# A quadrant-swapping copy in HBM: one queue of sixteen DMAs, or two queues of sixteen smaller ones

## The chip, the core and the metric

The kernel runs on one core of one Trainium2 chip. The metric is device time in microseconds for one execution. The core's instruction streams are those of TensorE (PE), VectorE (DVE), ScalarE (ACT), GpSimd (POOL) and SyncE (SP). Data between tensors in HBM is moved by the core's 16 DMA engines, which work through DMAs that one of the instruction streams has put on a queue.

## What is computed

```python
def setup_inputs():
    return {
        "x": np.random.randn(8192, 8192).astype(np.float32),
    }

def reference(x: np.ndarray) -> np.ndarray:
    return np.fft.ifftshift(x)
```

For an even size, `ifftshift` swaps the four quadrants of the matrix crosswise: the upper left quarter of the output is the lower right quarter of the input, the upper right is the lower left, and so on. Nothing is calculated. The matrix has 8192 rows of 32 KiB, 268.44 MB in all; each quadrant has 4096 rows, and a quadrant's part of a row is 4096 floats, 16 KiB, contiguous in memory. The next row of the same quadrant lies 32 KiB further on.

## The kernel before

The kernel consists of DMAs from the input in HBM straight to the output in HBM. The list `quads` (lines 23 to 28) names the four quadrants of the output, each with the quadrant of the input that it comes from. The outer loop (line 33) takes them in the order upper left, upper right, lower left, lower right. The inner loop (line 36) cuts each into `nsplit = 4` strips of 1024 rows, and line 41 issues one DMA for each strip: 16 DMAs of 1024 x 4096 floats, 16 MiB each.

`engines = [nc.sync]` (line 30) has one entry, so every DMA is issued by SP, in program order, on one queue. The other engines hold nothing but start and end barriers and, on POOL, four tiny constant fills.

The DMAs don't depend on each other. Tile, the layer in which the kernel is written, gives each a semaphore on which its landing is counted. There are eight of them, dealt out in turn, so the ninth DMA is issued only when the first has landed, the tenth when the second has, and so on. At the end of the program SP waits until the last DMAs have landed.

Of the kernel before, what the change touches and what calls it, by code (L numbers as in the profile page):

```python
# [1 line left out]

# [4 lines left out]


@with_exitstack  # L10
def kernel(
    ctx: ExitStack,
    tc: tile.TileContext,
    x: bass.AP,
    out: bass.AP,
):
    nc = tc.nc

    R, C = x.shape
    hr = R // 2  # L20
    hc = C // 2

    quads = [
        ((0, hr), (0, hc), (hr, R), (hc, C)),
        ((0, hr), (hc, C), (hr, R), (0, hc)),
        ((hr, R), (0, hc), (0, hr), (hc, C)),
        ((hr, R), (hc, C), (0, hr), (0, hc)),
    ]

    engines = [nc.sync]  # L30
    nsplit = 4
    k = 0
    for (or0, or1), (oc0, oc1), (ir0, ir1), (ic0, ic1) in quads:
        rows = or1 - or0
        step = rows // nsplit
        for s in range(nsplit):
            a = s * step
            b = a + step
            eng = engines[k % len(engines)]
            k += 1  # L40
            eng.dma_start(
                out=out[or0 + a : or0 + b, oc0:oc1],
                in_=x[ir0 + a : ir0 + b, ic0:ic1],
            )


# [1 line left out]
_INS = ['x']  # L48
_OUTS = [((8192, 8192), 'float32')]


def kernel(**inputs):
    import numpy as _np
    import concourse.bacc as _bacc
    import concourse.tile as _tile
    from concourse import mybir as _mybir
    from concourse.bass_utils import run_bass_kernel_spmd as _run

    nc = _bacc.Bacc("TRN2", target_bir_lowering=False, num_devices=1)  # L59
    arrays, args = {}, []  # L60
    for name in _INS:
        a = _np.ascontiguousarray(inputs[name])
        if a.dtype.kind in "iu":
            a = a.astype(_np.int64)
        arrays[f"in_{name}_dram"] = a
        args.append(nc.dram_tensor(f"in_{name}_dram", a.shape, _mybir.dt.from_np(a.dtype), kind="ExternalInput").ap())
    for i, (shape, dtype) in enumerate(_OUTS):
        dt = _mybir.dt.from_np(_np.dtype(dtype))
        args.append(nc.dram_tensor(f"out_{i}_dram", shape, dt, kind="ExternalOutput").ap())
    with _tile.TileContext(nc) as tc:  # L70
        kernel(tc, *args)
    r = _run(nc, [arrays], core_ids=[0])
    got = tuple(r.results[0][f"out_{i}_dram"] for i in range(len(_OUTS)))
    return got[0]
```

## Time and profile before

| What | Value |
|---|---|
| Median of 5 runs | 813.25 us (810.6 to 817.13) |
| The profiled execution, its own time | 813.76 us |
| The profiled execution, span from first to last instruction | 812.0 us |
| Instructions in the span | 61 |
| Busy time of compute engines | POOL 0.2 us, others none |
| DMA packets | 16,640 |

The page of the profile has a line `DMA` that shows how busy the 16 DMA engines were in each of 40 equal slices of the span (9 stands for 90% or more), and a line `GB/s` with what they moved in it, counted once for a byte that is read and written. A DMA is carried out as packets, and the part on the DMA queues gives for each queue its packets, their bytes in MB, and the time that the packets took, as a share of 16 engines over the whole span. The part on DMA issues gives, for each line of the kernel, the number of DMAs, the size of one, and the median time from issue to landing. Instructions that issue DMAs aren't counted as busy.

### The profile page before, as it was taken

Reading aid. Unit: us, or ns where it says so; the run is one execution under the profiler, and the core shown is the slowest. Engines: PE = TensorE matmul, PEld = TensorE weight load, DVE = VectorE, ACT = ScalarE, POOL = GpSimd, SP = SyncE. Lnnn points to the kernel's source line nnn. Section 1 sums busy time; section 2 is a strip of 40 time slices with the busy share of each in tenths; the row PEclk is TensorE's granted clock in tenths of the full one; section 3 lists DMA queues with packets and bytes.
Section 4 is the critical chain, followed back from the end, with each engine's and each line's share of the span. In section 5 each row is a group of like instructions: output and inputs, shape, how many; then the busy total and the mean of one; then the engine's idle time right before and its main releaser. Section 6 shows DMA issues by size and latency. Waiting matters only on the chain. (4 is left out here: it accounts for less than half of the span.)

```text
span 812.0 us, 61 instructions
## 1 busy us (share of the span) xinstructions
POOL 0.2 (0%) x4
## 2 busy tenths in 40 slices
POOL 0000000000000000000000000000000000000000
DMA  9999999999999999999999999999999999999998
GB/s 298 318 319 328 330 333 332 334 338 333 338 324 338 333 336 335 337 331 328 334 337 337 335 333 335 335 337 328 335 333 329 333 341 330 334 337 334 334 333 278
DMA packets 16640, 268.44 MB, mean 331 GB/s; under 512 B 256, under 2 KB 256, under 8 KB 256
## 3 DMA queue, kind: packets, MB, share of 16 engines
q1 hardware_dynamic: 16640, 268.44, 99.2%
HBM read 268.44 MB, written 268.44 MB: 661 GB/s over the span
## 5 line engine op out<-in xcount | busy, mean ns | idle before, releaser
L59 POOL MEMSET const-bfloat16-1.0<- 128x1 bf16 x1 | 0.1, 101 | 0.0
L59 POOL MEMSET const-uint8-127<- 128x1 uint8 x1 | 0.1, 101 | 0.0
L59 POOL MEMSET const-float32-0.0<- 128x1 f32 x1 | 0.1, 98 | 0.2 <-issue 0.2
L59 POOL MEMSET const-float32-1.0<- 128x1 f32 x1 | 0.1, 98 | 0.0
## 6 DMA issues: line engine op xcount, KB each, us to landing
out_dram<-in_x_dram SPq DMA_DIRECT2D x16, 16384.0 KB, 157.2
```

The costliest lines, as they stand in the source:

```text
L59: nc = _bacc.Bacc("TRN2", target_bir_lowering=False, num_devices=1)
```

## The change

The list of quadrants and the loop over it are replaced by a loop over strips of 512 rows of the upper half, and within it over the two column halves. Each step issues two DMAs. SP's writes 512 rows of the upper half of the output, from the lower half of the input. ScalarE's (`nc.scalar`) writes 512 rows of the lower half of the output, from the upper half of the input; where SP's writes the left columns it writes the right ones, and the other way round. A strip is 512 x 4096 floats, 8 MiB, and there are 32 DMAs, 16 on each of two queues.

```diff
+ROWS_PER_DMA = 512
...
-    quads = [
-        ((0, hr), (0, hc), (hr, R), (hc, C)),
-        ((0, hr), (hc, C), (hr, R), (0, hc)),
-        ((hr, R), (0, hc), (0, hr), (hc, C)),
-        ((hr, R), (hc, C), (0, hr), (0, hc)),
-    ]
-
-    engines = [nc.sync]
-    nsplit = 4
-    k = 0
-    for (or0, or1), (oc0, oc1), (ir0, ir1), (ic0, ic1) in quads:
-        rows = or1 - or0
-        step = rows // nsplit
-        for s in range(nsplit):
-            a = s * step
-            b = a + step
-            eng = engines[k % len(engines)]
-            k += 1
-            eng.dma_start(
-                out=out[or0 + a : or0 + b, oc0:oc1],
-                in_=x[ir0 + a : ir0 + b, ic0:ic1],
+    for row in range(0, hr, ROWS_PER_DMA):
+        for col in (0, hc):
+            other = hc - col
+            nc.sync.dma_start(
+                out=out[row : row + ROWS_PER_DMA, col : col + hc],
+                in_=x[row + hr : row + hr + ROWS_PER_DMA, other : other + hc],
+            )
+            nc.scalar.dma_start(
+                out=out[row + hr : row + hr + ROWS_PER_DMA, other : other + hc],
+                in_=x[row : row + ROWS_PER_DMA, col : col + hc],
             )
```

The eight landing semaphores are dealt out in turn over the DMAs of both queues: SP and ScalarE get four each, and from its fifth DMA on each of the two waits, before it issues, until the DMA that it issued four earlier has landed.

## The prediction

> **What bounds the kernel now.** No engine computes anything here, so I read the page's DMA lines first, then the DMA share by stretch of time, and then the waits of the sync engine's queue. The page:
>
> ```profile
> span 812.0 us, 61 instructions
> DMA  9999999999999999999999999999999999999998
> GB/s 298 318 319 328 330 333 332 334 338 333 338 324 338 333 336 335 337 331 328 334 337 337 335 333 335 335 337 328 335 333 329 333 341 330 334 337 334 334 333 278
> q1 hardware_dynamic: 16640, 268.44, 99.2%
> HBM read 268.44 MB, written 268.44 MB: 661 GB/s over the span
> out_dram<-in_x_dram SPq DMA_DIRECT2D x16, 16384.0 KB, 157.2
> ```
>
> One queue, q1, keeps the 16 DMA engines occupied for 99.2% of the span, and every slice but the last is at nine tenths or more. The chain of waits is of no use: it follows engine instructions and ends after 0.4 us. Of the 16,640 packets, 256 are the small ones that report a landing (16 DMAs on 16 engines); the other 16,384 carry 16 KiB each, one row of a quadrant, since 268.44 MB / 16,384 = 16,384 bytes. A packet therefore holds an engine for 0.992 x 16 x 812.0 / 16,384 = 0.787 us, which is 20.8 GB/s an engine and 333 GB/s for 16.
>
> Does something leave these engines without work, or do they work slower than they could? The windows (their first line names the columns):
>
> ```profile
> core 0: us, POOL busy (x), PEclk, DMA share, GB/s
> 0.00:5.00 5.00, 0.20 (x4) 1.00 0.61 223
> 5.00:20.00 15.00, 0.00 (x0) 1.00 1.00 321
> 20.00:60.00 40.00, 0.00 (x0) 1.00 1.00 319
> 60.00:110.00 50.00, 0.00 (x0) 1.00 0.99 330
> 110.00:160.00 50.00, 0.00 (x0) 1.00 1.00 333
> 210.00:410.00 200.00, 0.00 (x0) 1.00 1.00 333
> 610.00:790.00 180.00, 0.00 (x0) 1.00 1.00 334
> 805.00:812.00 7.00, 0.00 (x0) 1.00 0.55 176
> ...
> 3.00:4.00 1.00, 0.00 (x0) 1.00 1.01 426
> 302.00:303.00 1.00, 0.00 (x0) 1.00 1.09 426
> 305.00:306.00 1.00, 0.00 (x0) 1.00 0.74 279
> ```
>
> The share is 0.99 to 1.00 from 5 us to the tail, so no engine waits for descriptors, not even where one 16 MB DMA ends and the next begins. The last windows are of single microseconds: the rate swings between 279 and 426 GB/s while its mean stays at 333. The engines can thus run at 426 for a moment (26.6 GB/s an engine, 0.615 us a packet) and are held back to 0.787 us by something that they share. The stretch up to 60 us, in which all 16 have just started together, is the slowest: 319 to 321. The sync engine's own waits:
>
> ```profile
> SPq L70 <- DMA out_dram<-in_x_dram: 108.9, 3, 50.3
> ```
>
> These 108.9 us are its wait for the last landings. It issues far ahead (157.2 us from issue to landing, three DMAs of some 50 us). The issue takes nothing from the path.
>
> **What the Trainium skill says.** *HBM Reference*, Specifications: a pair of cores has about 716 GB/s of memory bandwidth. The trace's 661 GB/s, read and written together, is 92% of that, which agrees with memory, not the engines, as the shared limit. *DMA: Bandwidth & Descriptors*, "Issuing engines are not separate DMA queues": DMAs from scalar and sync run on the same 16 engines and interleave, and a second issuer saves only sequencer time. This trace has one issuer and can't show interleaving; it does show that there is no sequencer time to save. The same page, "Queues, rings and completion order": an engine takes turns between the rings that have work, a packet at a time. The same page, "Latency and other measured facts": streams that run in lock step with address pitches of large powers of two lose bandwidth (164 GB/s a direction at a pitch of 2 MiB, 207 at 512 KiB). No run here shows a pitch, but the slow first 60 us is what one would see if engines in step disturbed each other.
>
> **The change, part by part.**
> - Bytes and packets. Every output quadrant is still copied from the opposite one in rows of 16 KiB: 16,384 data packets, the same 268.44 MB each way. Landing packets go from 256 to 512 (32 DMAs x 16 engines). I take such a packet as under 0.1 us, since the share shows no dip at DMA ends; 16 more an engine are then at most 1.6 us, probably far less: 0 to +1.6, taken as +0.2.
> - Sync engine. It issues 16 DMAs of 8 MB in place of 16 of 16 MB. They lie beside the transfers now and do so after. Without that cover each issue would cost about 0.6 us (the first in the trace took 0.58), some 9 us in all.
> - Scalar engine. It gets 16 issues on a queue that was empty. The one thing exposed is its first issue, and until it has packets the sync ring feeds all 16 engines: 0.
> - Added waits. The eight landing semaphores are dealt out in turn over both issuers, so each has four, and its fifth DMA waits until its first has landed (before: the ninth for the first). Behind it in that queue stand only later DMAs. Three DMAs of 32 packets an engine are still queued in each ring, together 6 x 32 x 0.787 = 151 us of work. Cost 0; if it failed, one refill of about 2 us (the trace's first data moved at 2 us) at each of 12 waits would be 24 us, yet the other ring would have to be dry as well.
> - End. The rings share each engine, so one ending first leaves the whole engine to the other. The tail (share 0.55 over 7 us: 3.2 us) stays.
> - Order of addresses. This is the part that the trace of before can't price. Now all engines read one quadrant and write one; an engine's successive packets are 32 KB apart in both. After, an engine alternates between two quadrants read and two written, 128 MiB and one 16 KiB half row apart, and the block of one engine within a DMA (if rows are divided evenly and in order) falls from 64 rows, 2 MiB, to 32 rows, 1 MiB. Bound below: memory at the page's full 716 GB/s moves 536.9 MB in 750 us, and with what the engines don't fill (0.8% of 812.0: 6.5 us) it ends at 756. Bound above, by the nearest row, the 319 GB/s of the disturbed start held throughout: 268.44 / 0.319 = 841.5, and 6.5 makes 848. I take +1 us: the memory is already at 92% with 16 packets moving at once, and 16 still move at once whichever ring they come from; a slight loss is likelier to me than a gain, as four regions are open in place of two.
>
> Sum: 812.0 + 0.2 + 1 = 813.2 for the span. What lies around it is 813.76 - 812.0 = 1.8 us, so 815. The profiled run is 0.5 us above the median of 813.25, which is less than the spread of the five runs; I leave 815.
>
> **The rivals.**
> 1. *More open regions, worse memory efficiency: slower.* For: the engines already swing from 279 to 426[...], and a start in step costs 4% (319 against 333), so order matters. Against: after 110 us the mean is within 1% in every quadrant. It decides once the steady rate falls below 329 GB/s. Price: half way from 333 to 319 is 326, so 823.4 + 6.5 + 1.8 = 832.
> 2. *Two rings break the step: faster.* The rings place neighbouring packets in other halves of the memory, the start loses its slow 60 us, and the whole run keeps the best slice of the page, 341 GB/s. Price: 787.2 + 6.5 + 1.8 = 796. For: the headroom up to 426 exists at the engines. Against: 92% of the memory's stated rate leaves little, and the start alone is worth only (333 - 319) / 333 x 60 = 2.5 us.
> 3. *A ring runs dry* at a semaphore wait. It needs both rings dry at once; I give it nothing of its own and leave it in the tail of the first.
>
> **How the numbers follow.** About 0.5%, 4 us, is what a measurement of this kernel can tell from none: its five runs lie within 0.4% to 0.5% of their median. Memory-bound and unchanged, 815: 0.42, within which 0.30 falls inside 0.5%, 0.07 slower, 0.05 faster. Slower, near 832: 0.34. Faster, near 796: 0.24. So faster 0.29, same 0.30, slower 0.41. The range leaves out about one in ten at each end: 790 (a rate of 343.5) to 838 (a rate of 323.5). The likeliest case alone would be 808 to 822.
>
> **What would show it.** Two queues with half of the packets each, together 99% of the engines; a page rate of 331 to 333 in the middle slices; the sync and scalar queues waiting for landings without any dip in the DMA line. If the added waits cost, slices fall below nine tenths every 50 us. If rival 1 holds, the share stays at 1.00 and the middle slices read 326 or less; if rival 2, 338 or more, from the second slice on. I am wrong if the mean time of a packet moves by more than 0.5% in either direction, since nothing else in the kernel has weight.

## The result and the profile after

| | Before | After |
|---|---|---|
| Median, runs side by side | 815.75 us (78 runs) | 812.99 us (43 runs) |
| Ratio, 95% interval | | 0.997 (0.9958 to 0.9981) |
| Span of the profiled execution | 812.0 us | 811.7 us |

The changed kernel is faster by 0.3%, some 2.5 us of 815. Single executions of either kernel scatter by more than that (before: 810.5 to 824.0 us), so two profiled spans can't show the gain; the medians do. The page of the changed kernel:

```profile
span 811.7 us, 77 instructions
DMA  9999999999999999999999999999999999999998
GB/s 300 336 332 326 340 335 328 333 332 332 335 333 336 333 333 333 337 330 333 329 332 333 333 332 335 331 327 340 333 329 326 335 333 331 332 334 335 334 325 291
q1 hardware_dynamic: 8448, 134.22, 50.5%
q10 hardware_dynamic: 8448, 134.22, 48.8%
HBM read 268.44 MB, written 268.44 MB: 661 GB/s over the span
out_dram<-in_x_dram SPq DMA_DIRECT2D x16, 8192.0 KB, 201.6
out_dram<-in_x_dram ACTq DMA_DIRECT2D x16, 8192.0 KB, 201.8
```

There are two queues with half of the bytes each, together 99.3% of the engines' time, and the same 661 GB/s. They are served side by side: in the trace q1 moves 505 packets from 10 to 60 us and q10 501. In the line of slices, look at the second and third: 336 and 332, where before had 318 and 319. From the fifth on there is nothing to tell the two apart. The same by windows, of the changed kernel:

```profile
5.00:20.00 15.00, 0.00 (x0) 1.00 1.01 331
20.00:60.00 40.00, 0.00 (x0) 1.00 1.00 332
60.00:110.00 50.00, 0.00 (x0) 1.00 1.00 333
210.00:790.00 580.00, 0.00 (x0) 1.00 1.00 333
```

The start is as fast as the rest. Before, it was 321, 319 and 330, and later this:

```profile
210.00:790.00 580.00, 0.00 (x0) 1.00 1.00 334
```

Weighing those three by the rate of 334 gives (1 - 321/334) x 15 + (1 - 319/334) x 40 + (1 - 330/334) x 50 = 0.6 + 1.8 + 0.6 = 3.0 us lost, and after, by 333, 0.2 us. The difference is about the size of the gain. In these two executions most of it is lost again later, since the one of before runs at 334 for 580 us and the one of after at 333, which is 1.7 us: another reason to go by the medians. The waits of the sync engine's queue, after:

```profile
SPq L64 <- DMA out_dram<-in_x_dram: 165.1, 2, 117.8
SPq L31 <- DMA out_dram<-in_x_dram: 131.0, 12, 50.4
```

The twelve added waits are there (line 31) and take 131.0 us of the issuing queue, yet no slice of the DMA line falls for them. For ScalarE's queue the same view lists no waits; that it has twelve as well follows from the program and isn't shown.

### The profile page after: what moved, and what is told of

It is laid out like the page before. It is cut to its first block, busy times and chain, and to the rows that moved or that the text cites. A ratio compares the mean times of both kernels' runs of the same rounds, so it can differ in the third digit from the quotient of the medians.

```text
span 811.7 us, 77 instructions
## 1 busy us (share of the span) xinstructions
POOL 0.2 (0%) x4
```

## The experiments

Every ratio is to the kernel before, run on the same chip. The chips differ by about 1% (medians of before from 815 to 825 us), so each start below is compared with the later rate of its own execution: GB/s from 5 to 60 us, from 60 to 110, and from 210 to 790. A ratio isn't exactly the quotient of two medians (e15: 0.9915, where the medians 810.26 and 815.06 us give 0.9941).

| Run | Queues | Ratio, 95% interval | 5-60 | 60-110 | 210-790 |
|---|---|---|---|---|---|
| before | 1 | | 319 | 330 | 334 |
| e4 before again | 1 | 1.0001 (0.9977 to 1.0026) | 322 | 326 | 330 |
| e1 strips of 512 | 1 | 1.0015 (0.9997 to 1.0034) | 320 | 322 | 330 |
| e5 strips of 1040 | 1 | 1.0009 (0.9988 to 1.0029) | 324 | 329 | 330 |
| e8 interleaved rows | 1 | 1.0016 (0.9998 to 1.0035) | 321 | 326 | 329 |
| e7 second queue late | 1, then 2 | 1.0043 (1.0025 to 1.0061) | 325 | 323 | 328 |
| after | 2 | 0.997 (0.9958 to 0.9981) | 332 | 333 | 333 |
| e17 after again | 2 | 0.9974 (0.9959 to 0.999) | 333 | 332 | 333 |
| e2 strips of 1024 | 2 | 0.9975 (0.9959 to 0.9992) | 331 | 331 | 329 |
| e3 old order | 2 | 0.9977 (0.9962 to 0.9993) | 331 | 327 | 329 |
| e6 second queue at first | 2, then 1 | 0.9971 (0.9954 to 0.9988) | 326 | 331 | 330 |
| e15 both queues in each strip | 2 | 0.9915 (0.9882 to 0.9949) | 335 | 334 | 334 |
| e16 the same again | 2 | 0.9938 (0.9916 to 0.9961) | 334 | 333 | 334 |

One execution was profiled in each row, and the ten windows of 50 us from 260 to 760 us of one execution differ by 1% to 3% (before: 331 to 337). So a single start proves little; all of them together say more. Ten executions begin on one queue (four of them follow below: e9, e10, e11 and e14), and their first 55 us run at 95.5% to 99.1% of their later rate. Seven begin on two queues and run at 98.8% to 100.6%. Only e7 and e6 overlap.

**Which part of the change matters.** The change mixes strip size, order, and the second queue. Three kernels take one each, and one repeats the kernel before.

```diff
-    nsplit = 4
+    nsplit = 8
```

> One queue in the old order, strips of 512 rows in place of 1024. The gain of the change is taken to be the slow start: 319 GB/s from 20 to 60 us before, 332 after, 2.5 us in all. Theory A (the size of a strip, and with it the distance between two engines' rows, decides how much engines in step disturb each other): the start reads 328 or more, ratio 0.997. Theory B (two queues break the step, whatever the strip): the start stays at 317 to 322, ratio 1.000. Theory C (the start is chance, and the gain lies elsewhere): no relation between start and ratio.

```diff
-ROWS_PER_DMA = 512
+ROWS_PER_DMA = 1024
```

> The changed kernel with strips of 1024 rows: two queues, upper and lower half at once. Theory B (two queues break the step): start 328 or more from 20 to 60 us, ratio 0.997. Theory A (strip size decides): start 317 to 322, ratio 1.000. Both together: in between.

```diff
-    engines = [nc.sync]
+    engines = [nc.sync, nc.scalar]
```

> The kernel before with its DMAs dealt out in turn to the sync and the scalar engine, 1024 rows, one quadrant at a time: two queues without the pairing of upper and lower half. If the second queue alone breaks the step (B): start 328 or more, ratio 0.997. If it takes the pairing of two quadrants: start near 319, ratio 1.000, or slower. Theory A: start near 319, ratio 1.000.

> The kernel before once more, to see whether the slow start belongs to it. Theories A and B: 317 to 322 GB/s from 20 to 60 us again, 332 to 335 from 110 us on, ratio 1.000. Theory C (chance): a start anywhere between 319 and 335.

Strips of 512 rows on one queue keep the slow start and the time. Two queues with strips of 1024 rows, and even two queues in the old order, one quadrant at a time, have a fast start and the whole gain. The slow start came back in the repeat of before (e4):

```profile
5.00:60.00 55.00, 0.00 (x0) 1.00 1.00 322
210.00:790.00 580.00, 0.00 (x0) 1.00 1.00 330
```

Two queues in the old order (e3) have none:

```profile
5.00:60.00 55.00, 0.00 (x0) 1.00 1.00 331
210.00:790.00 580.00, 0.00 (x0) 1.00 1.00 329
```

So it isn't chance. The second queue is what counts (theory B), not the size (A).

**Where the gain sits.** Only the second DMA goes to the scalar engine, or only every second DMA after the first 100 us does.

```diff
-            eng = engines[k % len(engines)]
+            eng = nc.scalar if k == 1 else nc.sync
```

> The kernel before with only its second DMA given to the scalar engine: two queues for about the first 105 us, one for the remaining 700. If the gain of two queues is all at the start: start at 99% or more of the later rate, ratio 0.9975 as with two queues throughout. If two queues gain a little all the time: 1.5 in 12 parts of it, ratio 0.9995 to 1.000.

```profile
5.00:60.00 55.00, 0.00 (x0) 1.00 1.00 326
210.00:790.00 580.00, 0.00 (x0) 1.00 1.00 330
```

One DMA on a second queue, at work from 5 to 107 us, gives the full gain, 0.9971. Its profiled start of 326 falls just short of the 99% that I had asked for (98.8% of 330); the verdict rests on the times. The reverse:

```diff
+            if k > 4 and k % 2:
+                eng = nc.scalar
...
+            if k == 2:
+                for o, oc, i, ic in ((1024, hc, 5120, 0), (5120, 0, 1024, hc),
+                                     (5120, hc, 1024, 0)):
+                    nc.sync.dma_start(
+                        out=out[o : o + 2049 : 2048, oc : oc + hc].rearrange("r (e c) -> e r c", e=16),
+                        in_=x[i : i + 2049 : 2048, ic : ic + hc].rearrange("r (e c) -> e r c", e=16),
+                    )
```

> The reverse: one queue for the first 100 us, then every second DMA on the scalar engine. Three small DMAs that write six rows a second time, and that the scalar engine waits for, hold it back; they add 96 packets of 1 KB, estimated at under 1 us. If the gain is all at the start: start at 96% to 98% of the later rate, ratio 1.000 to 1.001. If two queues gain all the time: ratio 0.998.

It has no gain from a second queue that comes late, but its ratio of 1.0043 is in neither expectation, and its start (325) is 99.1% of its own later rate, not 96% to 98%. Its later rate is the low one, 328, and its tail is longer; why is open. So this run doesn't prove the reverse. One thing in its trace fits: the second queue moves its first packet at 111 us, and the rate, 323 from 60 to 110 us, is 331 from 110 to 160.

**Is it the start of the program, or any common start?** A barrier after the eighth DMA lets all 16 engines run empty and start again in the middle, on one queue or on two.

```diff
+            if k == 8:
+                tc.strict_bb_all_engine_barrier()
```

> The kernel before with a barrier after its eighth DMA: the sync engine waits until all eight have landed, and the other eight start with all 16 engines empty. If the slow stretch belongs to a common start of the engines on one queue, whenever it comes: after the barrier (about 408 us) the next 55 us again run at 96% to 98% of the later rate, and the time grows by a gap of 4 to 6 us and by 1.5 to 2.5 us more, ratio 1.007 to 1.010. If it belongs to the beginning of the program (memory used for the first time, say): full rate right after the gap, ratio 1.004 to 1.007.

```diff
-            eng = engines[k % len(engines)]
+            if k == 8:
+                tc.strict_bb_all_engine_barrier()
+            eng = nc.scalar if k > 8 and k % 2 else nc.sync
```

> The same barrier, but after it every second DMA is issued by the scalar engine. If a common start on two queues isn't slow, whenever it comes: full rate in the 55 us after the gap, and 0.002 to 0.003 less in ratio than with one queue after the barrier. If the two queues help only at the beginning of the program: the same ratio as with one.

The windows around the second start, of the kernel that restarts on one queue. The last three lines are the stretches after it:

```profile
390.00:400.00 10.00, 0.00 (x0) 1.00 1.00 341
405.00:410.00 5.00, 0.00 (x0) 1.00 0.54 184
...
413.00:468.00 55.00, 0.00 (x0) 1.00 1.00 326
468.00:518.00 50.00, 0.00 (x0) 1.00 0.99 326
...
525.00:625.00 100.00, 0.00 (x0) 1.00 1.00 327
```

And of the one that restarts on two:

```profile
390.00:400.00 10.00, 0.00 (x0) 1.00 1.02 336
410.00:415.00 5.00, 0.00 (x0) 1.00 0.51 174
...
415.00:470.00 55.00, 0.00 (x0) 1.00 0.99 333
470.00:520.00 50.00, 0.00 (x0) 1.00 1.00 333
```

The share of 0.54 or 0.51 is the gap, in which no packet moves for 1.9 and 1.8 us. After it one queue moves 326 GB/s for another 105 us and is still at 327 up to 625 us; two queues move 333 at once. From the first packet after the gap to the last of all, one queue takes 408.4 us and two 406.0. Each of the two executions had begun with a slow start of its own (both 322 from 5 to 60 us, on one queue), so the kernels of the pair differ only after the gap. The times point the same way: 1.0106 (1.0059 to 1.0153, six runs) with one queue, 1.0046 (1.0027 to 1.0065, 22 runs) with two. The intervals barely overlap, and the difference is twice the 0.002 to 0.003 that was expected. So on one queue a start in the middle is slow like the first one; the beginning of the program is not the reason.

A common start of the engines isn't enough for a slow stretch. In every kernel with two queues from the start the second one moves its first packet some 3 us after the first one (in the changed kernel q1 at 2.09 us, q10 at 5.07), so there too all engines start together on one queue; the slow stretch doesn't follow once the second has joined. Untested is one queue that ScalarE issues alone: every run with a fast start has one queue of each issuer.

**What of the second queue does it?** My first answer was addresses: engines in step at unlucky distances. Four kernels on one queue are meant to change those distances or the step. Which engine gets which rows is taken from how each DMA is written; the traces hold no addresses.

```diff
+        for a, b in ((0, 1040), (1040, 2080), (2080, 3120), (3120, 4096)):
```

> One queue in the old order, strips of 1040 rows (the last of each quadrant 976), so that neighbouring engines' rows are 65 rows or 2 MiB and 32 KiB apart, not 64 rows or 2 MiB. Theory A2 (the slow start comes from engines that run in step at distances of a large power of two): the start, 5 to 60 us, reaches 99% or more of the rate from 210 to 790 us, as with two queues, ratio 0.9975. Theory B (it takes a second queue): the start stays at 96% to 98%, ratio 1.000.

```diff
-                out=out[or0 + a : or0 + b, oc0:oc1],
-                in_=x[ir0 + a : ir0 + b, ic0:ic1],
+                out=out[or0 + a : or0 + b, oc0:oc1].rearrange("(r e) c -> e r c", e=16),
+                in_=x[ir0 + a : ir0 + b, ic0:ic1].rearrange("(r e) c -> e r c", e=16),
```

> One queue in the old order; within each strip engine e gets rows e, e+16, e+32 and so on in place of a block of 64, so engines in step are 32 KiB apart in place of 2 MiB. Theory A2 (distances in step decide): start at 99% or more of the later rate, ratio 0.9975 or lower, and if collisions cost something later too, a steady rate above that of before by 1% or more. Theory B (it takes a second queue): start at 96% to 98%, ratio 1.000.

Rows 65 apart instead of 64, or 1 apart instead of 64, leave the start at 98% and the time where it was. The start of e5 may be a little better (324, then 329); its ratio isn't.

```diff
+            if k == 0:
+                q = hc // 4
+                for r, n in ((0, 8), (8, 4), (12, 2), (14, 2)):
+                    nc.sync.dma_start(out=out[r : r + n, 0:q], in_=x[hr + r : hr + r + n, hc : hc + q])
+                nc.sync.dma_start(out=out[0:16, q:hc], in_=x[hr : hr + 16, hc + q : C])
+                a = 16
```

> One queue, old order; rows 0 to 15 of the first strip are cut so that engines 0 to 1, 2 to 3 and 4 to 7 (if a DMA of few rows takes the lowest-numbered engines) get some extra packets of 4 KB first, about 0.2 us each, and reach the first full packet at other moments of a packet than engines 8 to 15. If it is the engines' packets beginning at the same moment that makes the start slow: start at 99% or more of the later rate, ratio 0.9975. If not: 96% to 98%, ratio 1.000 to 1.001.

```diff
+            if k == 0:
+                nc.sync.dma_start(
+                    out=out[0:64, 0:hc].rearrange("(r e) c -> e r c", e=8),
+                    in_=x[hr : hr + 64, hc:C].rearrange("(r e) c -> e r c", e=8),
+                )
+                a = 64
```

> One queue; the first 64 rows go to eight engines alone (8 packets each, 6.3 us of work), so that these begin the first strip about 6 us behind the other eight. If the engines' common position in their rows makes the start slow: start at 99% or more of the later rate; the total is no help, since eight engines also end late (estimated at up to 3 us, ratio 0.999 to 1.003). If it doesn't: start at 96% to 98%, ratio 1.002 to 1.005.

Both starts stay slow: 325 from 5 to 60 us, against 334 later. The ratios are 1.0035 (1.0015 to 1.0055) for e11, of which the five DMAs issued first explain some 3 us (only 38 GB/s in the first 5 us), and 1.0015 (0.9986 to 1.0044) for e14. But e11 tests nothing: in its trace the small packets are over by 4.5 us, and then all 16 engines begin the last of the five DMAs within 0.4 us of each other (4.81 to 5.21 us), closer than in the kernel before (2.10 to 2.66). The shift of e14 is there: eight engines finish the first strip at 52.5 to 53.1 us, the other eight at 56.8 to 57.3. So a shift of about 4 us between two halves of the engines, some five packets of 0.79 us, doesn't mend the start; smaller shifts are untested.

The last test gives both queues the very rows that one had. Each strip's even rows go to one, its odd rows to the other:

```diff
+            o = out[or0 + a : or0 + b, oc0:oc1].rearrange("(e r t) c -> t e r c", e=16, t=2)
+            i = x[ir0 + a : ir0 + b, ic0:ic1].rearrange("(e r t) c -> t e r c", e=16, t=2)
+            nc.sync.dma_start(out=o[0], in_=i[0])
+            nc.scalar.dma_start(out=o[1], in_=i[1])
```

> Every strip of 1024 rows is issued by both engines at once, the even rows by sync and the odd rows by scalar. An engine that takes turns between its two queues then meets the rows in the order in which the kernel before has them. If the second queue as such makes the start fast, whatever it reads: start (5 to 60 us) at 99% or more of the rate from 210 to 790 us, ratio 0.997. If it takes two distant regions: 96% to 98%, ratio 1.000.

Its page and windows:

```profile
GB/s 308 333 333 332 332 333 339 331 335 331 335 326 336 337 336 330 330 336 336 331 331 333 335 332 333 336 334 337 332 328 338 334 331 333 336 333 333 336 331 302
...
5.00:20.00 15.00, 0.00 (x0) 1.00 1.00 342
20.00:60.00 40.00, 0.00 (x0) 1.00 0.99 333
210.00:790.00 580.00, 0.00 (x0) 1.00 1.00 334
805.00:812.00 7.00, 0.00 (x0) 1.00 0.22 77
```

The start is at full rate with no second strip of memory involved, so it isn't the distance between two regions that makes two queues start fast. The order of the rows isn't quite that of before, though: the second queue begins 3 us later, so by an estimate from 0.79 us a packet an engine's even rows run about four packets ahead of its odd ones. This kernel also has the lowest median of all. It was run again, beside the changed kernel:

> The kernel with every strip on both queues, even and odd rows, once more, beside the changed kernel on one chip. If its lead is real: ratio 0.990 to 0.995, and below that of the changed kernel. If the first measurement was luck: 0.997, as the changed kernel.

> The changed kernel once more, beside the former: ratio 0.996 to 0.998, start at 99% or more of the later rate. If the gain was one of the chip it ran on: 0.999 to 1.001.

810.53 us against 813.12 us for the changed kernel and 815.05 us for before; the changed kernel's ratio was confirmed at 0.9974. From 805 us on, the share is 0.22 in e15 and 0.21 in e16, against 0.62 and 0.36 in the two profiles of the changed kernel, but that says mainly that these executions were over sooner. In the 10 us before its last packet ends, an engine of e15 or e16 is without work for 0.5 and 0.8 us on average, one of the changed kernel for 0.8 and 1.1 us, so the end can explain only a part of the 2.6 us. The runs show more: the changed kernel came down to 809.45 us, below the lowest of e16 (810.21), and up to 816.93. The lead lies in the slower executions that e16 doesn't have. Why it scatters less is open.

**An inconclusive pair.** One queue that alternates between two strips was built from small DMAs.

```diff
+            if k < 2:
+                o = out[0:2048, 0:hc].rearrange("(s e r) c -> r e s c", s=2, e=16)
+                i = x[hr : hr + 2048, hc:C].rearrange("(s e r) c -> r e s c", s=2, e=16)
+                for r in range(32 * k, 32 * k + 32):
+                    nc.sync.dma_start(out=o[r], in_=i[r])
+                k += 1
+                continue
```

> One queue; the first two strips go out as 64 DMAs of 2 x 16 rows, so that every engine alternates between two strips 32 MiB apart as it does with two queues, for the first 105 us. If it is the alternation of addresses that makes the start fast: start at 99% or more of the later rate, ratio 0.9975. If it takes a second queue as such: start at 96% to 98%, ratio 1.000.

```diff
+                o = out[0:2048, 0:hc].rearrange("(s e r t) c -> s r e t c", s=2, e=16, t=2)
+                i = x[hr : hr + 2048, hc:C].rearrange("(s e r t) c -> s r e t c", s=2, e=16, t=2)
+                for r in range(32):
+                    nc.sync.dma_start(out=o[k, r], in_=i[k, r])
```

> The first two strips again as 64 DMAs of 2 x 16 rows on one queue, but each engine's two packets of a DMA are neighbouring rows of one strip, in the order of the kernel before. If the 178 GB/s of the run with two strips came from the small size of its DMAs: about 180 GB/s up to 190 us again, 890 to 900 us. If it came from alternating between two strips 32 MiB apart on one queue: 315 to 333 GB/s, 815 to 825 us.

The windows of the small DMAs, first with two strips, then with one:

```profile
20.00:185.00 165.00, 0.00 (x0) 1.00 1.00 177
```

```profile
20.00:145.00 125.00, 0.00 (x0) 1.00 1.00 229
```

The times were 895.5 us (ratio 1.0965, 1.0908 to 1.1021) and, in one run, 857.15 us. Neither expectation for the second was met. DMAs of 512 KB were slow by themselves here (229 GB/s), and with the alternation slower still (177), so the pair says nothing about the start.

## Why the prediction was wrong, by its own steps

- *The forecast* was 815 us: no change to speak of, and slower (0.41) likelier than the same (0.30) or faster (0.29). Measured was 0.3% faster, well inside the range of 790 to 838 us, but with an interval (0.9958 to 0.9981) that lies wholly on the faster side. That 815 lies only 2 us from 812.99 is partly luck: it was built on a profiled run of 813.76 us, while the 78 runs of before beside the changed kernel have a median of 815.75, from which the same sum gives 817.
- *What bounds the kernel* held in so far as the steady rate is 333 to 334 GB/s with one queue or two. That memory sets this rate was argued and is still not shown. The 426 GB/s in a window of 1 us isn't a rate: the share there is 1.09, because a packet is counted whole where it starts. The headroom is real all the same, since single packets of 16 KiB take as little as 0.61 us.
- *Bytes, landing packets, first issue, added waits, end*: held as costs near zero. A landing packet takes 9 ns in the trace of after, so 16 more on an engine are 0.14 us, where 0.2 was taken. Sixteen more DMAs on one queue (e1) gave 1.0015, about 1.2 us (-0.2 to 2.8), which can't be told from nothing; the twelve waits left the DMA line at nine tenths.
- *The step that failed* is the effect of a second queue on the start. The sum has it in two terms: "Scalar engine", put at 0, and "Order of addresses", where it says "I take +1 us" and "a slight loss is likelier to me than a gain". In their place the runs show about -2.5 us, and it belongs to the second queue, not to the order: two queues in the old order have it (e3, 0.9977), and so has a kernel with a second queue for the first 107 us alone (e6, 0.9971). The number was in the text: rival 2 worked out that the start is worth "(333 - 319) / 333 x 60 = 2.5 us", and this was then used as an argument against the rival, because its price of 796 assumed the page's best slice for the whole run as well. The slow start should have been a term of its own in the sum: either the change removes it, or it doesn't.
- *The reason* for rival 2, "Two rings break the step", was that packets are placed in other halves of the memory. That isn't what counts: two queues in the same rows start fast (e15), and one queue with other distances or with half of its engines shifted starts slowly (e5, e8, e14). Of the rival's outcome the fast start came, the rate of 341 GB/s did not.
- *Rival 1*, more open regions: refuted for this pairing. Reading and writing two quadrants at once kept 333.
- *Its own sign of being wrong*, a mean packet time that moves by more than 0.5%, didn't appear: by the same working the changed kernel has 0.993 x 16 x 811.7 / 16,384 = 0.787 us, as before. The sign was too coarse for 0.3%, and a mean over the whole run hides the start, where 16 x 16,384 bytes at 319 and at 332 GB/s make 0.82 and 0.79 us a packet.
- *What the Trainium skill says* of a second issuer (*DMA: Bandwidth & Descriptors*, "Issuing engines are not separate DMA queues"), that it saves only sequencer time, holds for the steady part, and missed by 0.3% here, since no sequencer time was to be saved. Its note on address pitches (the same page, "Latency and other measured facts"), which calls lock step an inference, was the wrong guide to the slow start: no distance tried changed it. Nor is it right that "No run here shows a pitch": by the prediction's own division of the rows, neighbouring engines of the kernel before are 2 MiB apart, and it moved 333 GB/s, where the note has 164 for copies of another shape.

Open remains what makes one queue slow after a start of all engines. Shown is only that a second queue, in every order of the rows that was tried, removes it.

## What to carry to other kernels

A copy whose DMA engines are 99% busy can still have a slow stretch: read the rate by windows, set each stretch against the steady rate, and enter the loss into the sum as a term that the change may remove. Where one queue feeds long transfers, try giving two queues the same strips, even and odd rows: here it was worth 0.6% (810.53 against 815.05 us), twice what two queues in different quadrants brought. And don't take the busy share for speed.

## What was not expected of the hardware

- After all 16 engines start together and one queue alone goes on feeding them, the rate is mostly 2% to 4.5% low for some 100 us (319 against 334 at the worst), and for up to 200 us in e1 and e9, at the program's start and after a gap in the middle alike. With a second queue from the start it was at most 1.2% low (e6), in the other six profiles 0.3% or less.
- The DMA share stays at 1.00 while the rate falls to 177 or 229 GB/s (DMAs of 512 KB, two packets an engine). The share counts the whole time of a packet, however long it takes: 16 x 16,384 bytes at 177 GB/s make 1.48 us for a packet, at 333 GB/s 0.79.
- With both queues in the same rows the time of a kernel scatters less: 810.21 to 811.08 us in nine runs, against 809.45 to 816.93 us in 22 of the changed kernel and 811.97 to 820.85 us in thirty of before, on the same chip.
